# One layer of a hybrid attention block: the first two weight chunks laid out piece by piece, and the first input tile multiplied in two halves

## The chip, the cores and the metric

The kernel runs on one core of one Trainium2 chip. The metric is the device time of one execution in microseconds (us), the median over several runs; less is better. A profile of one execution shows what each engine did: PE is TensorE (PEld its weight loads), DVE VectorE, ACT ScalarE, POOL GpSimd, SP the engine that only issues transfers here. The engines run apart from each other and meet at semaphores; each takes its own instructions in a fixed order.

## What is computed

One layer for 512 frames of width 1024, in float32: a combined input projection, two kinds of attention, a gated mix, and a convolutional feed-forward part. The opening works on this piece of the reference:

```python
hn = rms_norm(x, norm1_g[l])
proj = hn @ w_in[l]
qa, ka, va = [proj[..., i * WIDTH_A:(i + 1) * WIDTH_A].reshape(b, s, N_HEADS_A, HEAD_DIM)
              for i in range(3)]
...
q = rms_norm(q, q_gain)
k = rms_norm(k, k_gain)
```

`w_in` has 1024 rows. A product over 1024 rows is summed over eight k tiles of 128 rows.

## The kernel before

**Precision.** Each float32 operand is split into a high part (rounded to the matmul's format) and a low part (the rest). A product takes three matmuls: high by high, high by low, low by high. For the input these parts are `hth` and `htl` (lines 385 and 386, ScalarE and VectorE, from `xs`), for weights `whi` and `wlo` (lines 278 to 281, from `raw`). In the trace `uA<-whi_uA,hth` is a matmul that adds to the bank uA with the weights' high part as moving data and the input's high part as stationary data.

**Chunks.** All weights are cut on the host into chunks of 128 x 2048 numbers (1 MB), in the order of their use (`_chunks`). The first two, `uA0` and `uA1`, hold the first four heads' columns of q and k: a chunk has four k tiles of 512 columns each, 256 of q and 256 of k. `uA0` has the k tiles 0 to 3, `uA1` 4 to 7. Then come `vA0`, `vA1` (the values), `qA1`, `kA1` and so on.

**Loading.** `load(i, parts)` issues a chunk's transfers on SP. In DRAM a chunk is `wts[i]`, 128 rows of 2048 numbers, 8 KB a row. A whole chunk goes as one transfer; the first two are loaded in four pieces of 512 columns (line 148), so that each partition takes 2 KB out of a row of 8 KB. The input is there transposed as `xt`, eight tiles of 128 x 512 (256 KB, contiguous). SP issues by turns one input tile (line 340) and one weight piece: xs 0, piece 0 of uA0, xs 1, piece 1, up to xs 7 and piece 3 of uA1. The rest of the parameters, the untransposed input `xtok` (2 MB, for the norms' factors) and the chunk `vA0` follow. A small load of the parameters that scale the input is issued on ScalarE's queue.

**Splitting.** `split_gen(i, pieces)` yields after each piece. The loop over k ahead of the first chunk takes one step of it for each input tile, so that the engines get, by turns, an input tile's parts and a weight piece's parts. The very first cast is VectorE's, all others are ScalarE's; all low parts are VectorE's. For later chunks `run_chunk` takes a step of the next chunk's split after each part of a chunk's matmuls. When a chunk is split, the load of the next but one is issued.

**Matmuls of the opening.** Nine warm-up matmuls on zeros (line 355) stand first on PE. Then `unit_groups` fills four banks of 128 frames x 512 columns (`pss[t]`, t = 0 to 3) from `uA0` and `uA1`. For `uA0` the k tile is the outer loop, then the three products, then the four banks: 12 matmuls of 512 columns for a k tile. For `uA1` the bank is the outer loop, and each bank is evacuated when it is full (`evac`: squares on ScalarE, a sum over 64 columns and factors on VectorE and GpSimd, then the normalized `n_uA`). `vA0` and `vA1` go the same way, through the same four banks; between their matmuls stand transposes of `n_uA` (line 574).

**Order.** The order of each engine's instructions is set when the program is built, by a scheduler with a model of time that takes ready work from several streams. A change of one instruction's size can so move others later on.

Of the kernel before, what the change touches and what calls it, by code (L numbers as in the profile page):

```python
# [8 lines left out]
F32 = mybir.dt.float32  # L9
F32R = mybir.dt.float32r  # L10
AF = mybir.ActivationFunctionType
ALU = mybir.AluOpType
# [3 lines left out]
P = 128  # L16
S = 512
D = 1024
NT = S // P
# [44 lines left out]

CHUNKS = _chunks()

SEVEN = (6, 7, 9, 10, 11, 12, 13, 15, 17)
LIVE = (17,)
EXTRA_AT = (7, 10, 12)
# [4 lines left out]
def block_kernel(ctx: ExitStack, tc: tile.TileContext, x, xt, params, g2, rbx, wts, wd0, wd1, out):  # L74
    nc = tc.nc
    V, A, G, PE, SP = nc.vector, nc.scalar, nc.gpsimd, nc.tensor, nc.sync
# [42 lines left out]
    FIRST_DN = order.index("dn0_0")  # L119
    keep = {}  # L120

    def load(i, parts=1):
        if i == FIRST_DN + 2:

            raw = late["hp"].tile([P, 2048], F32, tag="ax9", name="raw_dn0_2")
        else:
            raw = wp.tile([P, 2048], F32, tag="raw", name=f"raw_{order[i]}")
        raws[i] = raw
        if i >= FIRST_DN:
            n = i - FIRST_DN  # L130
            if n < NP:
                SP.dma_start(raw, wd0[n])
            else:
                late["load"] = (SP.dma_start(raw[:, 0:1024], wd1[n - NP]),)
            yield
            return

        if is_seven(i) and i - pos["up0"] not in LIVE:
            n = SEVEN.index(i - pos["up0"])
            SP.dma_start(raw[:, 0:512], wts[i, :, 0:512])  # L140
            SP.dma_start(raw[:, 512:1024], parked[n, :, 0:512])
            SP.dma_start(raw[:, 1024:2048], wts[i, :, 1024:2048])
            yield
            return
        cuts = [0, *parts, 8] if isinstance(parts, tuple) else [8 * j // parts for j in range(parts + 1)]
        for a, b in zip(cuts, cuts[1:]):
            sl = slice(256 * a, 256 * b)
            SP.dma_start(raw[:, sl], wts[i, :, sl])
            yield

    def chain(kind, ins):
# [34 lines left out]
    def is_seven(i):  # L186
        return i < len(order) and order[i] in [f"up{j}" for j in SEVEN]

    def park_gen():

        for j in SEVEN:
            if j in LIVE:
                continue
            n = SEVEN.index(j)
            i = pos[f"up{j}"]
# [17 lines left out]
    def block_sums(i):  # L213

        b = raws[i].rearrange("p (b c) -> p b c", c=512)
        sx = late["pool"].tile([P, 1536], F32, tag="sx", name=f"sx_{order[i]}")
        late["sx"] = sx
        s1, s2, s4 = (sx[:, 512 * j:512 * (j + 1)] for j in range(3))
        for o, x, y, op in ((s1, b[:, 1], b[:, 3], ALU.add), (s2, s1, b[:, 0], ALU.subtract),
                            (s4, b[:, 2], s2, ALU.subtract), (b[:, 1], b[:, 0], b[:, 1], ALU.subtract)):  # L220
            V.tensor_tensor(o, x, y, op=op)
            yield

    def fetch_extra(j):

        n = SEVEN.index(j)
        if j in EXTRA_AT:
            wh, wl = (t[:, 16:1552] for t in late["w2"])
        else:
            wh, wl = (late["pool"].tile([P, 1600], F32R, tag=tag, name=f"{tag}_up{j}")[:, 16:1552]  # L230
                      for tag in ("wxh", "wxl"))
        SP.dma_start(wh.bitcast(F32), parked[n, :, 512:2048])
        SP.dma_start(wl.bitcast(F32), parked[n, :, 2048:3584])
        extras[j] = wh, wl
# [21 lines left out]
    def split_gen(i, pieces):  # L256

        if i >= len(order):
            return
        key = order[i]  # L260
        kn = CHUNKS[i][1]
        raw = raws.pop(i)
        if i - pos["up0"] in LATE and i - pos["up0"] not in LIVE:
            fetch_extra(i - pos["up0"])
        sh = 48 if key[:2] in ("qA", "kA", "vB") else 16 if key in ("up0", "up1") or is_seven(i) else 0
        n = 512 * kn if i >= FIRST_DN else 2048
        hi = wp.tile([P, 2112], F32R, tag="whi", name=f"whi_{key}")[:, sh:sh + n]
        lo = wp.tile([P, 2112], F32R, tag="wlo", name=f"wlo_{key}")[:, sh:sh + n]
        splits[key] = (hi.rearrange("p (k c) -> p k c", k=kn), lo.rearrange("p (k c) -> p k c", k=kn))
        if i >= FIRST_DN:  # L270
            yield from split_down(i - FIRST_DN, raw, hi, lo)
        elif is_seven(i):
            yield from split_seven(i, raw, hi, lo)
        n = 2048 // pieces
        for j in range(pieces if i < FIRST_DN and not is_seven(i) else 0):
            sl = slice(n * j, n * (j + 1))
            if i == 0 and j == 0:
                V.tensor_copy(hi[:, sl], raw[:, sl])
            else:
                A.copy(hi[:, sl], raw[:, sl])  # L280
            V.tensor_tensor(lo[:, sl], raw[:, sl], hi[:, sl].bitcast(F32), op=ALU.subtract)  # L281
            if j < pieces - 1:
                yield


        nxt = {0: None, 1: i + 3, 2: None}.get(i - FIRST_DN, i + 2)
        if nxt is not None and nxt < len(order):
            next(load(nxt))
        j = i + 1 - pos["up0"]
        if j in SEVEN and j not in LATE:  # L290
            fetch_extra(j)
        yield
        if j in LIVE:
            yield from block_sums(i + 1)
# [17 lines left out]
    hth = hp.tile([P, NK, S], F32R, tag="hth", name="hth")  # L312
    htl = hp.tile([P, NK, S], F32R, tag="htl", name="htl")
# [21 lines left out]

    pieces = (p for i in range(2) for p in load(i, 4))
    for k in range(NK):
        SP.dma_start(xs[:, k, :], xt[k])  # L340
        next(pieces)
    for _ in pieces:
        pass
    SP.dma_start(par[:, 8:N_PAR], params[:, 8:N_PAR])
# [9 lines left out]
    for i in range(WARM):  # L354
        PE.matmul(pw.rearrange("p (a b) -> p a b", a=4), warm, warm.unsqueeze(1).to_broadcast([P, 4, P]),
                  start=True, stop=True)
# [70 lines left out]
    def unit_groups(hi, lo, key, evac):  # L427

        unit, half = key[:-1], int(key[-1])
        if half == 0:  # L430
            open_banks[unit] = [(MM if t else PV)(f"{unit}_{t}") for t in range(NT)]
        pss = open_banks[unit]

        def mm(t, k, j):
            st, mv = ((hth, hi), (hth, lo), (htl, hi))[j]
            PE.matmul(pss[t], st[:, 4 * half + k, t * P:(t + 1) * P], mv[:, k, :], start=half == 0 and k == 0 and j == 0,  # L436
                      stop=half == 1 and k == 3 and j == 2, skip_group_check=True)
        if key == "uA0":
            for k in range(4):
                for j in range(3):  # L440
                    for t in range(NT):
                        mm(t, k, j)
                yield
            return
        for t in range(NT):
            for k in range(4):
                for j in range(3):
                    mm(t, k, j)
            if half == 1:
                evac(t, pss[t])  # L450
            yield
# [387 lines left out]
    for s in range(len(steps)):  # L839
# [8 lines left out]
        br, h, t, e = pend.pop(0)  # L848
# [33 lines left out]
    n = 0  # L882
# [67 lines left out]
    hi, lo = splits.pop("wo3")  # L950
# [401 lines left out]
def _layout(inputs):  # L1352
    import numpy as np
    f = {k: np.asarray(v) for k, v in inputs.items()}
    x = f["x"]
    g = f["q_norm_g"][0]
    k = f["k_norm_g"][0]
    params = np.concatenate([
        f["norm1_g"].reshape(NK, P), np.concatenate([g, g])[None], np.concatenate([k, k])[None],
        f["ffn_conv_w"].reshape(3 * 2 * NF, P), f["ffn_conv_b"].reshape(2 * NF, P)], axis=0).T  # L1360

    idx = np.clip(np.arange(639) - 127, -128, 128) + 128
    rbx = f["rel_bias"][0][:, idx]
    wts = np.empty((len(CHUNKS) - 2 * NP, P, 2048), np.float32)
    for i, (key, kn, parts) in enumerate(CHUNKS[:-2 * NP]):
        views = [f[name][0][r0:r0 + kn * P, c0:c0 + n] for name, r0, c0, n in parts]
        w = views[0] if len(views) == 1 else np.concatenate(views, axis=1)
        if key in [f"up{j}" for j in SEVEN]:

            a = w.reshape(2, 4, P, 2, P).transpose(0, 3, 2, 1, 4)  # L1370
            wts[i] = np.concatenate([a[k, f].reshape(P, 512) for k in range(2) for f in range(2)], axis=1)
            continue
        wts[i] = w.reshape(kn, P, 2048 // kn).transpose(1, 0, 2).reshape(P, 2048)

    w = f["w_ffn_down"][0].reshape(NP, 2, P, 2, 512)
    wd0 = np.concatenate([w[:, 0, :, 0], w[:, 1, :, 0], w[:, 0, :, 1], w[:, 1, :, 1]], axis=2)
    wd1 = np.concatenate([w[:, 1, :, 1], w[:, 1, :, 0]], axis=2)
    arrays = {"x": x, "xt": x[0].T.reshape(NK, P, S),
              "params": params, "g2": f["norm2_g"], "rbx": rbx, "wts": wts, "wd0": wd0, "wd1": wd1}
    return {n: np.ascontiguousarray(a) for n, a in arrays.items()}  # L1380
# [15 lines left out]
```

## Time and profile before

| | us |
|---|---|
| median of 3 runs | 722.66 |
| the three runs | 721.46, 722.66, 722.86 |
| the profiled execution | 721.76 |
| its span, first to last instruction | 720.1 |
| PE busy | 712.3 |
| VectorE busy | 588.6 |
| ScalarE busy | 409.7 |

The span is 1.7 us shorter than the profiled execution's own time; that rest lies around the instructions. Busy time of PE is the sum of matmuls as recorded; matmuls overlap a little, so it is no measure of distance from the peak. In rows of a timeline the columns are: start, length, engine, line, operation, output and inputs, shape, count, and in brackets the engine's idle time ahead of it with what ended it. In rows of a window: the window, then busy time of PE, PEld, DVE, ACT and POOL (with counts), the granted clock of PE, the mean busy share of the DMA engines, and what they moved in GB/s, which is also KB per us. Rows of transfers give destination and source, the issuing queue, the count, the size of one, and the median us from issue to landing.

### The profile page before, as it was taken

How to read it: one execution, taken by the hardware profiler on the slowest of the kernel's cores; microseconds unless marked ns; L12 is line 12 of the kernel's file. 1: busy time of each engine (PE TensorE's matmuls, PEld its weight loads, DVE VectorE, ACT ScalarE, POOL GpSimd, SP SyncE). 2: the span in 40 equal slices, each digit the busy share in tenths (PEclk: the TensorE clock that was granted, in tenths of full speed). 3: DMA queues.
4: the chain of work that ended last, by engine and by line, in shares of the span. 5: the costliest groups of instructions: out<-in, count | busy, mean ns of one | idle time of the engine just before them, and what ended most of it. 6: DMA issues, size and time to landing. Idle time of an engine off the chain costs nothing.

```text
span 720.1 us, 10786 instructions
## 1 busy us (share of the span) xinstructions
PE 712.3 (99%) x3971; PEld 619.0 (86%) x3971; DVE 588.6 (82%) x1050; ACT 409.7 (57%) x755; POOL 54.9 (8%) x91
## 2 busy tenths in 40 slices
PE   8999999999999999999999999999999999999997
PEld 6889998888988888878889988999988988888885
DVE  6668878796998999869556698998999985998686
ACT  6666656667776677545335554666655543543531
POOL 2501200000110111100003000000000100000000
PEclk9999999999999999999999999999999999999999
DMA  9722235434434443554937837667765633564553
GB/s 303 269 106 88 76 129 187 179 133 180 157 148 160 176 162 147 192 190 172 335 124 287 264 117 257 247 230 289 250 248 204 227 130 115 185 244 167 181 214 117
DMA packets 38469, 136.59 MB, mean 190 GB/s; under 512 B 4112, under 2 KB 8592, under 8 KB 30864
## 3 DMA queue, kind: packets, MB, share of 16 engines
q1 hardware_dynamic: 35472, 122.66, 47.7%
q0 software_dynamic: 2656, 13.11, 4.9%
q8 instruction: 31, 0.51, 0.3%
q14 instruction: 22, 0.18, 0.1%
q10 hardware_dynamic: 288, 0.14, 0.1%
HBM read 109.41 MB, written 26.48 MB: 189 GB/s over the span
## 4 chain that ended last, share of the span: by engine, by line
PE 96%; DVE 2%; DMA 1%; ACT 0%; issue 0%; SPq 0%; DVEq 0%; ACTq 0%
PE P L1232 15%; PE p L1138 12%; PE pg L309 3%; PE pg L307 3%; PE pg L308 3%; PE pu L309 3%; PE pu L307 3%; PE pu L308 3%; PE uA L436 3%; PE vA L436 3%; PE qkB L309 2%; PE gB L307 2%; PE qkB L307 2%; PE qkB L308 2%; PE gB L308 2%; PE gB L309 2%
## 5 line engine op out<-in xcount | busy, mean ns | idle before, releaser
L1232 PE MATMUL P<-whi_dn,ax 128*128 128x512 f32 x176 | 54.4, 389 | 0.0
L165 ACT CAST whi_dn<-raw_dn 128x1024 fp32r<-128x1024 f32 x33 | 34.4, 1052 | 25.4 <-PE P L1232 11.1
L161 DVE TENSOR_TENSOR wlo_dn<-raw_dn,whi_dn 128x1024 fp32r<-128x1024 f32 x33 | 40.0, 1223 | 7.7 <-ACT whi_dn L165 7.7
L309 PE MATMUL pg<-hth,wlo_up 128*128 128x512 f32 (+1 forms) x120 | 43.3, 361 | 0.0
L307 PE MATMUL pg<-hth,whi_up 128*128 128x512 f32 (+1 forms) x120 | 43.2, 361 | 0.0
L308 PE MATMUL pg<-htl,whi_up 128*128 128x512 f32 (+1 forms) x120 | 43.2, 360 | 0.0
L308 PE MATMUL pu<-htl,whi_up 128*128 128x512 f32 (+1 forms) x116 | 41.6, 359 | 0.0
L307 PE MATMUL pu<-hth,whi_up 128*128 128x512 f32 (+1 forms) x116 | 41.6, 359 | 0.0
L309 PE MATMUL pu<-hth,wlo_up 128*128 128x512 f32 (+1 forms) x116 | 41.6, 358 | 0.0
L1232 PE MATMUL P<-whi_dn,ay 128*128 128x512 f32 x132 | 40.8, 389 | 0.0
L1232 PEld LDWEIGHTS P<-whi_dn,ax 128*128 128x128 f32 x176 | 33.0, 188 | 6.8
L207 ACT CAST pkh<-pkr 128x512 fp32r<-128x512 f32 x24 | 14.9, 621 | 38.5 <-DMA parked<-pkh 16.5
L281 DVE TENSOR_TENSOR wlo_up<-raw_up,whi_up 128x1024 fp32r<-128x1024 f32 (+1 forms) x32 | 31.3, 1022 | 4.7 <-ACT whi_up L280 4.7
L1232 PE MATMUL P<-wlo_dn,ax 128*128 128x512 f32 x88 | 34.2, 389 | 0.0
L280 ACT CAST whi_up<-raw_up 128x1024 fp32r<-128x1024 f32 (+1 forms) x32 | 26.5, 886 | 10.6 <-PE pu L308 5.8
L741 POOL TENSOR_SCALAR_AFFINE_SELECT bB<-bB 128x128 f32<-128x128 f32 x32 | 18.7, 592 | 151.6 <-DVE bB L740 132.3
L1232 PEld LDWEIGHTS P<-whi_dn,ay 128*128 128x128 f32 x132 | 24.8, 188 | 5.1
L739 DVE TENSOR_TENSOR_SCAN aB<-aB,reset 128x127 f32<-128x127 f32 (+3 forms) x32 | 25.7, 815 | 4.1 <-ACT aB L734 4.1
L208 DVE TENSOR_TENSOR pkr<-pkr,pkh 128x512 fp32r<-128x512 f32 x24 | 16.5, 687 | 12.3 <-ACT pkh L207 12.3
L307 PE MATMUL gA<-hth,whi_gA 128*128 128x512 f32 x64 | 25.5, 399 | 0.3 <-DVE mixA L619 0.3
L1232 PE MATMUL P<-wlo_dn,ay 128*128 128x512 f32 x66 | 25.8, 391 | 0.0
L1138 PE MATMUL p<-ts,whi_up 128*128 128x256 f32 x144 | 25.5, 277 | 0.0
(317 smaller groups left out, 2395.3 us busy)
## 6 DMA issues: line engine op xcount, KB each, us to landing
raw_up<-in_wts SPq DMA_DIRECT2D x14, 1024.0 KB, 5.2
raw_dn<-in_wd SPq DMA_DIRECT2D x11, 1024.0 KB, 4.8
pkr<-in_wts SPq DMA_DIRECT2D x8, 1024.0 KB, 6.7
parked<-pkr SPq DMA_DIRECT2D x32, 256.0 KB, 2.9
parked<-pkh SPq DMA_DIRECT2D x24, 256.0 KB, 2.0
raw_dn<-in_wd SPq DMA_DIRECT2D x11, 512.0 KB, 3.3
ayd<-ay POOLq DMA_DIRECT2D x7, 768.0 KB, 6.2
ay<-ayd POOLq DMA_DIRECT2D x7, 768.0 KB, 6.0
```

The lines of the kernel that those rows point to most:

```text
L161: chain("halves", V.tensor_tensor(o, x, y, op=op))
L165: chain("casts", A.copy(hi[:, sl], src))
L280: A.copy(hi[:, sl], raw[:, sl])
L281: V.tensor_tensor(lo[:, sl], raw[:, sl], hi[:, sl].bitcast(F32), op=ALU.subtract)
L307: PE.matmul(ps, sh, mh, start=first, stop=False)
L308: PE.matmul(ps, sh, ml, start=False, stop=False)
L309: PE.matmul(ps, sl, mh, start=False, stop=last)
L436: PE.matmul(pss[t], st[:, 4 * half + k, t * P:(t + 1) * P], mv[:, k, :], start=half == 0 and k == 0 and j == 0, stop=half == 1 and k == 3 ...
L739: V.tensor_tensor_scan(ar, ar, reset[:, S - n:S - 1][:, ::-1], 1.0, op0=ALU.mult, op1=ALU.max)
L741: G.affine_select(b[:, n - P:n], b[:, n - P:n], pattern=[[-1, P]], compare_op=ALU.is_gt, fill=0.0, base=0, channel_multiplier=1)
L1138: PE.matmul(ps, st, mv[:, k, :], start=first and k == 0 and n == 0, stop=last and k == 3 and n == 2, skip_group_check=True)
L1232: chain("products", PE.matmul(dst, st, mv, start=first and n == 0, stop=last and n == 2, skip_group_check=True))
```

## The change

Three things are changed. On the host, the numbers of chunks 0 and 1 are laid out in DRAM piece by piece, each piece contiguous (`CUTS` has the cuts). `load` reads each piece as one contiguous region; the row that a partition takes has 2 KB as before. The first piece of chunk 0 is cut in two, the 256 columns of q and the 256 columns of k of k tile 0, each a transfer of its own (128 KB, 1 KB for a partition); SP issues both behind the first input tile. Split and matmuls follow: VectorE casts the q half, ScalarE the k half, VectorE makes two low parts; and the matmuls of k tile 0 have 256 columns, 24 in place of 12, in the order high q, high k, low q, input's low part with q, with k, low k. All other chunks are loaded and split as before.

```diff
+CUTS = ((0, 256, 512, 1024, 1536, 2048), (0, 512, 1024, 1536, 2048))
...
-    def load(i, parts=1):
+    def load(i):
...
-        cuts = [0, *parts, 8] if isinstance(parts, tuple) else [8 * j // parts for j in range(parts + 1)]
-        for a, b in zip(cuts, cuts[1:]):
-            sl = slice(256 * a, 256 * b)
-            SP.dma_start(raw[:, sl], wts[i, :, sl])
+        for c0, c1 in zip(CUTS[i], CUTS[i][1:]) if i < 2 else ((0, 2048),):
+            src = bass.AP(wts.tensor, (2048 * i + c0) * P, [[c1 - c0, P], [1, c1 - c0]])
+            SP.dma_start(raw[:, c0:c1], src)
             yield
...
-        for j in range(pieces if i < FIRST_DN and not is_seven(i) else 0):
-            sl = slice(n * j, n * (j + 1))
+        cuts = CUTS[0] if i == 0 else [n * j for j in range(pieces + 1)] if i < FIRST_DN and not is_seven(i) else ()
+        for j, sl in enumerate(map(slice, cuts, cuts[1:])):
             if i == 0 and j == 0:
                 V.tensor_copy(hi[:, sl], raw[:, sl])
             else:
                 A.copy(hi[:, sl], raw[:, sl])
-            V.tensor_tensor(lo[:, sl], raw[:, sl], hi[:, sl].bitcast(F32), op=ALU.subtract)
-            if j < pieces - 1:
-                yield
+                if i == 0 and j == 1:
+                    yield
+                    V.tensor_tensor(lo[:, 0:256], raw[:, 0:256], hi[:, 0:256].bitcast(F32), op=ALU.subtract)
+            if (i, j) != (0, 0):
+                V.tensor_tensor(lo[:, sl], raw[:, sl], hi[:, sl].bitcast(F32), op=ALU.subtract)
+                if j < len(cuts) - 2:
+                    yield
...
-    pieces = (p for i in range(2) for p in load(i, 4))
+    pieces = (p for i in range(2) for p in load(i))
     for k in range(NK):
         SP.dma_start(xs[:, k, :], xt[k])
         next(pieces)
+        if k == 0:
+            next(pieces)
...
         if key == "uA0":
-            for k in range(4):
+            for j, c in ((0, 0), (0, 256), (1, 0), (2, 0), (2, 256), (1, 256)):
+                for t in range(NT):
+                    st, mv = ((hth, hi), (hth, lo), (htl, hi))[j]
+                    PE.matmul(pss[t][:, c:c + 256], st[:, 0, t * P:(t + 1) * P], mv[:, 0, c:c + 256],
+                              start=(j, c) == (0, 0), stop=False, skip_group_check=True)
+            yield
+            for k in range(1, 4):
...
+        if i < 2:
+
+            wts[i] = np.concatenate([wts[i][:, a:b].ravel() for a, b in zip(CUTS[i], CUTS[i][1:])]).reshape(P, 2048)
```

Where the instructions now stand, at three places. In the rows below, L is a line of the kernel that the rows belong to, the name ahead of the arrow is written and those behind it are read; the number at a name's end tells buffers apart.

VectorE in the opening, before: the cast of the first weight piece, the first input tile's low part, that piece's low part, and the next two.

```order
L278 CAST whi_uA_159<-raw_uA_119 128x512
L386 SCALAR_TENSOR_TENSOR htl<-xs,par,hth 128x512
L281 TENSOR_TENSOR wlo_uA_160<-raw_uA_119,whi_uA_159 128x512
L386 SCALAR_TENSOR_TENSOR htl<-xs,par,hth 128x512
L281 TENSOR_TENSOR wlo_uA_160<-raw_uA_119,whi_uA_159 128x512
```

And in the changed kernel:

```order
L279 CAST whi_uA_160<-raw_uA_119 128x256
L284 TENSOR_TENSOR wlo_uA_161<-raw_uA_119,whi_uA_160 128x256
L393 SCALAR_TENSOR_TENSOR htl<-xs,par,hth 128x512
L286 TENSOR_TENSOR wlo_uA_161<-raw_uA_119,whi_uA_160 128x256
L393 SCALAR_TENSOR_TENSOR htl<-xs,par,hth 128x512
L286 TENSOR_TENSOR wlo_uA_161<-raw_uA_119,whi_uA_160 128x512
```

Cast and low part of the first piece are halved; the q half's low part stands ahead of the input's low part, the k half's behind it.

ScalarE in the opening, before: two input tiles, then the second weight piece's cast.

```order
L95 DMA par<-in_params 128x8
L96 ACT_TABLE_LOAD
L385 ACTIVATE hth<-xs,par 128x512 x2
L280 CAST whi_uA_159<-raw_uA_119 128x512
L385 ACTIVATE hth<-xs,par 128x512
```

In the changed kernel the k half's cast stands between the first two input tiles:

```order
L97 DMA par<-in_params 128x8
L98 ACT_TABLE_LOAD
L392 ACTIVATE hth<-xs,par 128x512
L281 CAST whi_uA_160<-raw_uA_119 128x256
L392 ACTIVATE hth<-xs,par 128x512
L281 CAST whi_uA_160<-raw_uA_119 128x512
```

So the second input tile's part (and with it everything behind it on ScalarE) now waits for the k half too.

VectorE where uA's banks are evacuated and vA0 is split, before: `n_uA` is a bank's normalized q and k, `wlo_vA_306` the low parts of vA0 in four pieces, `ss_uA` a sum of squares.

```order
L466 TENSOR_TENSOR n_uA<-uA_221,rs_uA_301 128x2x256
L281 TENSOR_TENSOR wlo_vA_306<-raw_vA_175,whi_vA_305 128x512
L403 TENSOR_SCALAR cols<-cols 128x1
L281 TENSOR_TENSOR wlo_vA_306<-raw_vA_175,whi_vA_305 128x512 x3
L466 TENSOR_TENSOR n_uA<-uA_222,rs_uA_325 128x2x256
```

And in the changed kernel, where the pieces are `wlo_vA_321`:

```order
L479 TENSOR_TENSOR n_uA<-uA_224,rs_uA_316 128x2x256
L286 TENSOR_TENSOR wlo_vA_321<-raw_vA_180,whi_vA_320 128x512
L410 TENSOR_SCALAR cols<-cols 128x1
L286 TENSOR_TENSOR wlo_vA_321<-raw_vA_180,whi_vA_320 128x512
L475 TENSOR_REDUCE ss_uA_360<-sq_uA_358 128x8
L286 TENSOR_TENSOR wlo_vA_321<-raw_vA_180,whi_vA_320 128x512
L479 TENSOR_TENSOR n_uA<-uA_225,rs_uA_340 128x2x256
L286 TENSOR_TENSOR wlo_vA_321<-raw_vA_180,whi_vA_320 128x512
```

A sum of squares and the second bank's normalization moved ahead of the last pieces. Shifts of this kind, with the same instructions in another order, go on for PE, VectorE and ScalarE through the first attention heads, and end at the first matmuls of the chunk `kA1`; from there on the orders agree to the end. GpSimd's order is the same, and SP's has the one more transfer.

## The prediction

> **What bounds the kernel now.** I read the page's table of busy time first, then its chain that ended last, then the waits of the matmul engine over the whole span. They say that TensorE is the bound nearly everywhere, and that the opening is the one place where it stands still for long.
>
> ```profile
> PE 712.3 (99%) x3971; PEld 619.0 (86%) x3971; DVE 588.6 (82%) x1050; ACT 409.7 (57%) x755; POOL 54.9 (8%) x91
> ...
> PE 96%; DVE 2%; DMA 1%; ACT 0%; issue 0%; SPq 0%; DVEq 0%; ACTq 0%
> ...
> PE uA L436 <- DVE whi_uA L278: 1.3, 1, 1.3
> PE warm L355 <- DVE warm L352: 1.1, 1, 1.1
> PE yB L308 <- DVE ol_B L793: 0.4, 1, 0.4
> ```
>
> The reader is to see that after the opening no single wait of PE is longer than 0.4 us. So what the opening gains or loses is handed on to the end almost whole: every later engine and load follows PE, and PE has no slack of its own. Next comes the chain in order of time, in its first pieces.
>
> ```profile
> 0.80 0.39 SPq L340
> ...
> 1.25 4.82 DMA raw_uA<-in_wts
> 6.08 0.44 DVE whi_uA L278
> 6.52 0.14 issue
> 6.66 22.30 PE uA L436 x96
> ```
>
> The first 256 KB of weights are issued at 1.25 and land at 6.07; a VectorE copy of 0.44 and 0.14 of hand-over follow, and PE starts its first useful matmul at 6.66. From there its 96 matmuls of uA run through. The timeline of PE shows what lies ahead of that start and how the first k tile goes:
>
> ```profile
> 1.11 4.21 PE L355 MATMUL warm<-warm 128*128 128x512 f32 x9 [1.11 <-DVE warm L352]
> ...
> 4.69 0.63 PE L355 MATMUL warm<-warm 128*128 128x512 f32 x1
> ...
> 6.66 1.18 PE L436 MATMUL uA<-whi_uA,hth 128*128 128x512 f32 x4 [1.33 <-DVE whi_uA L278]
> 7.83 1.19 PE L436 MATMUL uA<-wlo_uA,hth 128*128 128x512 f32 x4
> 8.85 1.07 PE L436 MATMUL uA<-whi_uA,htl 128*128 128x512 f32 x4
> 9.76 1.07 PE L436 MATMUL uA<-whi_uA,hth 128*128 128x512 f32 x4
> ```
>
> Nine warm-up matmuls start from 1.11 to 4.69, (4.69 - 1.11)/8 = 0.45 us apart; those of uA start (9.76 - 8.85)/4 = 0.227 us apart. So PE runs at half pace at first and is at full pace later, whatever the page's row of granted clock (9 in every slice) says. The first k tile takes 9.76 - 6.66 = 3.10 instead of 12 x 0.227 = 2.72, since its second group waits for VectorE. The second k tile starts at 9.76: this is the mark by which I measure.
>
> The timelines of ScalarE and VectorE give what the first k tiles wait for.
>
> ```profile
> 3.69 0.72 ACT L385 ACTIVATE hth<-xs,par 128x512 fp32r<-128x512 f32 x1 [1.17 <-DMA par<-in_params]
> 6.79 0.73 ACT L385 ACTIVATE hth<-xs,par 128x512 fp32r<-128x512 f32 x1 [2.38 <-DMA xs<-in_xt]
> 8.29 0.62 ACT L280 CAST whi_uA<-raw_uA 128x512 fp32r<-128x512 f32 x1 [0.77 <-DMA raw_uA<-in_wts]
> ...
> 6.08 0.43 DVE L278 CAST whi_uA<-raw_uA 128x512 fp32r<-128x512 f32 x1 [5.02 <-DMA raw_uA<-in_wts]
> 6.43 0.75 DVE L386 SCALAR_TENSOR_TENSOR htl<-xs,par,hth 128x512 fp32r<-128x512 f32 x1
> 7.09 0.69 DVE L281 TENSOR_TENSOR wlo_uA<-raw_uA,whi_uA 128x512 fp32r<-128x512 f32 x1
> ```
>
> The first input tile is ready at 3.69 + 0.72 = 4.41, so only the weights are late. The next input tile lands at 6.79 and the next weight piece at 8.28.
>
> **The change part by part.** *When the weights land.* Three views bear on it: landing times of the first transfers, the same of line 140 (later in the kernel, 256 KB cut as 2 KB out of rows of 8 KB like today's pieces, ahead of its group), and the bytes moved in each microsecond.
>
> ```profile
> xs<-in_xt SPq DMA_DIRECT2D x1, 256.0 KB, 2.7
> raw_uA<-in_wts SPq DMA_DIRECT2D x1, 256.0 KB, 4.8
> ...
> L140 SPq DMA_DIRECT2D raw_up<-in_wts x8: 328/332/333, 424.1 to 510.9; - x8
> ...
> DMA to landing us min/median/max: 3.4/4.0/6.4
> ...
> 2.00:3.00 1.00, 1.00 (x4) 0.71 (x4) 0.00 (x0) 0.52 (x1) 0.93 (x2) 1.00 0.76 235
> 3.00:4.00 1.00, 1.00 (x4) 0.81 (x3) 0.00 (x0) 0.32 (x1) 0.94 (x2) 1.00 1.31 222
> 4.00:5.00 1.00, 1.00 (x4) 0.50 (x2) 0.00 (x0) 0.41 (x1) 0.67 (x2) 1.00 0.69 113
> 5.00:6.00 1.00, 0.32 (x1) 0.00 (x0) 0.00 (x0) 0.00 (x0) 0.00 (x0) 1.00 1.01 213
> 6.00:7.00 1.00, 0.34 (x2) 0.32 (x3) 0.92 (x2) 0.21 (x1) 0.00 (x0) 1.00 0.99 324
> ```
>
> The input tile, contiguous in DRAM, lands 2.7 after its issue, at 3.50. Cut pieces of the same size need 3.4 at best, 4.0 in the middle and 6.4 at worst. And while the first cut piece is under way the DMA engines are busy (0.69 to 1.31) but move 113 to 222 KB per us, against 324 later: they wait inside packets. I take it that the cut layout costs this. Contiguous, 128 KB behind the input tile's 256 KB at 222 KB per us land at 3.50 + 0.6 = 4.1; the bounds are 3.9 (at 324) and 6.07 (nothing gained). The second half follows by 4.7. The next input tile and weight piece bring the sum to 1049 KB; today 1107 KB have moved between 2.00 and 7.00, so these land by about 7.2, if no DMA engine lags, against 8.28.
>
> Of the Trainium skill a rule speaks against this: Perfetto Trace Analysis, Contiguity and DMAs, holds that contiguity counts only within one SBUF partition's line, and that is 2 KB before and after for all pieces but the halved one. By that rule the landing stays as it is, which is the first rival below; the rows of line 140 against the input tile's speak against the rule, without settling it, since other transfers stand around them.
>
> *When PE starts.* With a landing at 4.1, the cast of half the columns costs between 0.43/2 and 0.43, and the hand-over 0.14: ready by 4.7 at the latest. But the ninth warm-up starts at 4.69, and PE takes its work in order: the first useful matmul starts at 4.69 + 0.45 = **5.14**. The warm-up is what is late next; the landing has some 0.4 us of slack behind it.
>
> *The first k tile.* 24 matmuls of 256 columns take the place of 12 of 512. Their pace comes from qA, the same operands at 256 columns: 13 matmuls in the chain, of which the first and last are
>
> ```profile
> 54.85 0.12 PE qA L307
> ...
> 56.27 0.12 PE qA L307
> ```
>
> 1.42/12 = 0.118 each, so 24 x 0.118 = 2.83, 0.11 more than 2.72. VectorE now makes low part, input's low part, low part; the low part of the first half is ready some 0.4 after its cast, and PE asks for it 8 matmuls after its start, so the wait inside the tile goes. PE is at half pace at 4.69 and at full pace by 8.85, and at which moment it changes no row shows. With the change at 5.14 nothing is lost, with the change at 6.66 (6.66 - 5.14)/2 = 0.76; I take the middle, 0.38. The tile ends at 5.14 + 2.83 + 0.38 = **8.35**. Bounds: 7.97 and 8.73. The second k tile needs its cast by then: a landing at 7.2, 0.62 and 0.14 give 7.96. That fits.
>
> A sentence of the Trainium skill, TensorE: Matmul & The Clock Gate, Part 1, puts the change of pace after a free-running window of about 3.4 us of activity, so from 1.11 on between 4.5 and 7.9: an estimate by that page loses up to (7.9 - 5.14)/2 = 1.4 instead of 0.76.
>
> *Costed at nothing.* One more issue on SP moves every later one back by 1.72 - 1.25 = 0.47:
>
> ```profile
> 1.25 0.42 SPq L148 DMA_DIRECT2D raw_uA<-in_wts  x1
> 1.72 0.42 SPq L340 DMA_DIRECT2D xs<-in_xt  x1
> ```
>
> These transfers wait behind others for longer than that; were they not to, the second input tile would land 0.47 later than worked out, and its slack (PE needs it at 8.35) covers it. ScalarE's one more cast and VectorE's one more subtraction stand in a stage where each needs about 1.4 us for a k tile and PE 2.72. The order of PE, VectorE and ScalarE also differs up to kA's first matmuls, a tenth of the span from its start; there PE waits for nothing now, so reordering can gain nothing there, and it may cost.
>
> **The sum.** 9.76 - 8.35 = **1.41** us (bounds 9.76 - 8.73 = 1.03 and 9.76 - 7.97 = 1.79). Against the profiled execution, 721.76: 720.35. That execution lies 0.90 under the median of 722.66, and the three runs spread over 1.4 us. If that spread comes from this same landing (line 140's spreads from 3.4 to 6.4), the change takes it away too and the time stays at 720.35; if not, it is 722.66 - 1.41 = 721.25. I take the middle: **720.8**.
>
> **The rivals.** *The layout gives nothing (0.23).* The cut rows are not what stalls the DMA engines; the second half lands at 6.07, the next piece at 8.28. PE has the q half early, but its matmuls of the k half stand second in its queue. Second half: 6.07 + ScalarE's cast of 0.4 + 0.14 = 6.61; 20 matmuls x 0.118 end at 8.97; the second k tile needs 8.28 + 0.62 + 0.14 = 9.04. Gain 9.76 - 9.04 = 0.72, time 722.66 - 0.72 = 721.94. For it: in 4 to 6 us contiguous input tiles are in the queue too, and the slow stretch holds them as well.
>
> *The gain is given back at vA (0.08).* In VectorE's new order a reduction and a normalization stand ahead of the last low part of vA0.
>
> ```profile
> 27.50 1.89 DVE L281 TENSOR_TENSOR wlo_vA<-raw_vA,whi_vA 128x512 fp32r<-128x512 f32 x3
> 29.30 0.68 DVE L466 TENSOR_TENSOR n_uA<-uA,rs_uA 128x512 f32<-128x512 f32 x1
> 29.90 1.27 DVE L462 TENSOR_REDUCE ss_uA<-sq_uA 128x8 f32<-128x512 f32 x2
> ...
> 31.33 0.39 PE L436 MATMUL vA<-wlo_vA,hth 128*128 128x512 f32 x1
> ```
>
> Today it is done at 29.39 and wanted at 31.33. Behind 0.68 + 0.64 it is done at 30.71. If PE comes 1.41 earlier and VectorE not, PE waits 30.71 - 29.92 = 0.79, and 0.62 of the gain is left: 722.04. Against it: VectorE's work there hangs on PE's uA banks and moves along.
>
> *The second half late: slower (0.04).* The matmuls of the k columns stand ahead of all others in the queue, so PE ends the first k tile no sooner than the second half's landing + 0.54 + 20 x 0.118 = landing + 2.90. It is slower than today from a landing at 6.86. With the longest landing among the weight pieces of the opening, 6.9 after issue,
>
> ```profile
> DMA to landing us min/median/max: 4.8/5.8/6.9
> ```
>
> it would land at 1.72 + 6.9 = 8.62, the tile end at 11.52, 1.76 later than now: 724.4.
>
> **How the numbers follow.** My forecast has 0.65, with a range of its own from 719.9 (full pace at once, spread gone: 721.76 - 1.79 = 719.97) to 721.6 (722.66 - 1.03). The layout rival reaches up to 721.94, the vA rival to 722.04; the range is 719.9 to 722.2. A measurement of this kernel can tell about 0.2%, 1.44 us, from no change: faster means under 721.22. Of my forecast some 0.50 lies under it, of the layout rival 0.03 (where the spread goes); slower is the last rival. So 0.53 faster, 0.43 the same, 0.04 slower.
>
> **What would show it.** In the new profile the first 256-column matmul should start at about 5.1 with no wait behind the warm-ups, the first weight piece land by 4.6, the second k tile start near 8.35, and the stretch from 3 to 6 us move over 250 KB per us. If the first landing is still near 6, the layout was not the cause. If the second k tile starts early but uA's last matmul does not end some 1.4 us before 28.96, the gain is lost between; if it does and the whole is not shorter, in the reordered stretch up to kA. I am wrong if the DMA engines still stall, or if PE stays at half pace past 6.7 us.

## The result, and the profile after

| | before | after |
|---|---|---|
| median of the runs | 722.66 (7 runs, 721.46 to 723.23) | 720.05 (7 runs, 719.62 to 721.15) |
| ratio, 95% interval | | 0.9971 [0.9961, 0.9982] |
| the profiled execution | 721.76 | 719.62 |
| its span | 720.1 | 717.9 |

The kernel is faster by 2.61 us at the median and by 2.14 us between the two profiled executions. The ratio, which is not the quotient of these two medians (0.9964), gives 2.1 us, with an interval from 1.3 to 2.8. Forecast were 720.8, a range of 719.9 to 722.2, and a gain of 1.41. The sign holds and the time lies in the range, near its low end.

The page of the profile after: the row of busy times, and the chain's shares by engine.

```profile
PE 711.6 (99%) x3983; PEld 619.6 (86%) x3983; DVE 588.6 (82%) x1051; ACT 410.0 (57%) x756; POOL 55.2 (8%) x91
...
PE 97%; DVE 2%; ACT 0%; issue 0%; DVEq 0%; ACTq 0%
```

DMA has left the chain; PE's busy time is much as it was. What went is a wait. The matmul engine's waits after:

```profile
PE warm L362 <- DVE warm L359: 1.1, 1, 1.1
PE yB L313 <- DVE ol_B L806: 0.4, 1, 0.4
```

The 1.3 us of uA on the first cast are gone, and no new wait is in its place. PE's timeline of the opening after:

```profile
1.12 4.21 PE L362 MATMUL warm<-warm 128*128 128x512 f32 x9 [1.12 <-DVE warm L359]
5.13 1.23 PE L449 MATMUL uA<-whi_uA,hth 128*128 128x256 f32 x8
6.19 0.64 PE L449 MATMUL uA<-wlo_uA,hth 128*128 128x256 f32 x4
6.67 1.12 PE L449 MATMUL uA<-whi_uA,htl 128*128 128x256 f32 x8
7.63 0.64 PE L449 MATMUL uA<-wlo_uA,hth 128*128 128x256 f32 x4
8.11 1.09 PE L443 MATMUL uA<-whi_uA,hth 128*128 128x512 f32 x4
```

The first useful matmul follows the warm-ups at 5.13, and the second k tile starts at 8.11, not 9.76. What the weights do is read from the casts that take them, on VectorE and on ScalarE:

```profile
4.17 0.65 DVE L279 CAST whi_uA<-raw_uA 128x256 fp32r<-128x256 f32 x1 [3.11 <-DMA raw_uA<-in_wts]
```

```profile
5.08 0.41 ACT L281 CAST whi_uA<-raw_uA 128x256 fp32r<-128x256 f32 x1 [0.40 <-DMA raw_uA<-in_wts]
6.52 0.72 ACT L392 ACTIVATE hth<-xs,par 128x512 fp32r<-128x512 f32 x1 [1.03 <-DMA xs<-in_xt]
7.32 0.62 ACT L281 CAST whi_uA<-raw_uA 128x512 fp32r<-128x512 f32 x1
```

The q half is there at 4.17 and the k half at 5.08. The next piece waits for nothing but ScalarE, so it had landed by 7.32. In the windows of the same stretch,

```profile
4.00:5.00 1.00, 1.00 (x4) 0.57 (x3) 0.80 (x2) 0.68 (x1) 0.67 (x2) 1.00 0.81 223
5.00:6.00 1.00, 1.00 (x8) 1.00 (x8) 1.00 (x3) 0.41 (x1) 0.00 (x0) 1.00 1.02 346
```

the DMA engines move 223 and 346 GB/s where they moved 113 and 213. In second profiles of the two kernels, used further down, it is 174 and 326 against 109 and 260.

Where the 2.14 us come from shows in the chain in order of time. Two pieces of it after: vA's first matmul, and the first long run of p, a 256-column product of the feed-forward part.

```profile
27.34 0.23 PE vA L443
...
446.62 14.63 PE p L1151 x129
```

And of before:

```profile
28.96 0.24 PE vA L436
...
448.32 14.86 PE p L1138 x129
```

At vA the gain is 28.96 - 27.34 = 1.62; from there to p both take the same, 419.28 and 419.36. Then the same 129 matmuls take 0.23 less. So the opening's gain travels 419 us almost unchanged, and some 0.4 us more come up behind 446 us, in matmuls that the change doesn't touch.

### The profile page after: what moved, and what is told of

It is laid out like the page before. It is cut to its first block, busy times and chain, and to the rows that moved or that the text cites. A ratio compares the mean times of both kernels' runs of the same rounds, so it can differ in the third digit from the quotient of the medians.

```text
span 717.9 us, 10814 instructions
## 1 busy us (share of the span) xinstructions
PE 711.6 (99%) x3983; PEld 619.6 (86%) x3983; DVE 588.6 (82%) x1051; ACT 410.0 (57%) x756; POOL 55.2 (8%) x91
## 4 chain that ended last, share of the span: by engine, by line
PE 97%; DVE 2%; ACT 0%; issue 0%; DVEq 0%; ACTq 0%
PE P L1245 15%; PE p L1151 12%; PE pg L313 3%; PE pg L312 3%; PE pg L314 3%; PE pu L313 3%; PE pu L314 3%; PE pu L312 3%; PE vA L443 3%; PE uA L443 3%; PE qkB L314 2%; PE gB L312 2%; PE qkB L312 2%; PE qkB L313 2%; PE gB L313 2%; PE gB L314 2%
```

## The experiments

Runs of each kernel were taken by turns with runs of the kernel before on the same chip. The first four (`layout_only`, `split_only`, `pitch`, `warm13`) were compared together, then three more (`pitch_8448`, `pitch_32k`, `early`), then `pitch_8192`, each comparison on another chip. The ratio alone is not enough here: the runs of the kernel before fall mostly into two groups, 720.7 to 721.8 and 722.0 to 723.9. In the upper one were 16 of 26 runs in the first comparison, 12 of 28 in the second and 4 of 13 in the third, so its median was 722.62, 721.47 and 721.36, and ratios of different comparisons can't be set side by side. So each kernel is also read by marks in its profile: the cast of the next weight piece on ScalarE, the start of the second k tile on PE, and the first vA matmul.

| kernel | rows of chunks 0, 1 | next piece | 2nd k tile | vA | profiled | median | ratio |
|---|---|---|---|---|---|---|---|
| before | 8 KB | 8.29 | 9.76 | 28.96 | 721.76 | 722.66 | |
| before_again | 8 KB | 7.83 | 9.50 | 28.70 | 721.06 | | |
| before_third | 8 KB | 8.04 | 9.31 | 28.51 | 720.90 | | |
| split_only | 8 KB | 8.73 | 9.40 | 28.75 | 721.42 | 721.05 | 0.9981 [0.9972, 0.9990] |
| split_again | 8 KB | 7.63 | 8.45 | 27.68 | 719.98 | | |
| pitch_8192 | 8 KB, apart | 8.28 | 8.96 | 28.30 | 722.08 | 720.66 | 0.9982 [0.9971, 0.9992] |
| pitch_8448 | 8.25 KB, apart | 7.02 | 8.86 | 28.12 | 721.01 | 720.38 | 0.9976 [0.9965, 0.9986] |
| pitch | 9.25 KB, apart | 7.01 | 8.32 | 27.55 | 719.72 | 720.08 | 0.9969 [0.9956, 0.9982] |
| pitch_32k | 32 KB, apart | 7.52 | 8.59 | 27.82 | 720.12 | 720.16 | 0.9979 [0.9970, 0.9989] |
| layout_only | contiguous pieces | 6.91 | 8.37 | 27.57 | 719.97 | 720.17 | 0.9971 [0.9961, 0.9982] |
| after | contiguous pieces | 7.32 | 8.11 | 27.34 | 719.62 | 720.05 | 0.9971 [0.9961, 0.9982] |
| after_again | contiguous pieces | 7.07 | 8.14 | 27.37 | 719.71 | | |
| early | contiguous pieces | 7.02 | 7.84 | 27.07 | 719.30 | 720.23 | 0.9978 [0.9969, 0.9987] |
| warm13 | contiguous pieces | 6.54 | 8.62 | 27.85 | 721.84 | 722.80 | 1.0008 [0.9997, 1.0019] |

Times are us; "apart" is a DRAM tensor of its own that holds only chunks 0 and 1.

**The layout alone.** The kernel before, with its four pieces and its matmuls, but the pieces of chunks 0 and 1 contiguous.

```diff
             sl = slice(256 * a, 256 * b)
-            SP.dma_start(raw[:, sl], wts[i, :, sl])
+            if i < 2:
+                n = 256 * (b - a)
+                src = bass.AP(wts.tensor, (2048 * i + 256 * a) * P, [[n, P], [1, n]])
+            else:
+                src = wts[i, :, sl]
+            SP.dma_start(raw[:, sl], src)
```

> The kernel before with chunks 0 and 1 contiguous by piece in DRAM and nothing else: four pieces of 512 columns, 12 matmuls of 512 columns for the first k tile, the order of every engine as before. If the cut rows stalled the DMA engines (layout theory): the first piece (256 KB, behind 256 KB of input) lands at 4.6 to 4.9 instead of 6.07, PE starts at 5.2 to 5.5, the second k tile at 8.3 to 8.6 instead of 9.76, the time falls by 1.1 to 1.4 us. If the split did it (rival): the piece lands near 6, the second k tile starts at 9.4 to 9.8, the time falls by 0 to 0.3 us.

VectorE's first cast and PE's first and second k tile:

```profile
4.32 0.62 DVE L283 CAST whi_uA<-raw_uA 128x512 fp32r<-128x512 f32 x1 [3.26 <-DMA raw_uA<-in_wts]
```

```profile
5.12 1.57 PE L441 MATMUL uA<-whi_uA,hth 128*128 128x512 f32 x4
6.53 1.09 PE L441 MATMUL uA<-wlo_uA,hth 128*128 128x512 f32 x4
...
8.37 1.07 PE L441 MATMUL uA<-whi_uA,hth 128*128 128x512 f32 x4
```

The whole first piece lands at 4.32, earlier than the 4.6 to 4.9 expected, and the warm-ups are what PE starts behind, as after the full change. PE waits for no weights up to the second k tile. Its first four matmuls take 6.53 - 5.12 = 1.41 where full pace gives 4 x 0.227 = 0.91: 0.50 goes to half pace. The ratio is that of the full change, with the same interval. The orders of the engines are those of before, so the reordering is worth nothing that shows.

**The halves alone.** The changed kernel's pieces, casts and orders, but read out of rows of 8 KB as before.

```diff
-            src = bass.AP(wts.tensor, (2048 * i + c0) * P, [[c1 - c0, P], [1, c1 - c0]])
-            SP.dma_start(raw[:, c0:c1], src)
+            SP.dma_start(raw[:, c0:c1], wts[i, :, c0:c1])
```

> The changed kernel with the old layout in DRAM: the halves of the first piece and all other pieces are cut out of rows of 8 KB; the order of every engine as in the changed kernel. Layout theory: the q half lands at 5.0 to 5.6 instead of 4.17, the k half near 6, the next weight piece near 8 instead of 7.31, and the second k tile starts at 8.8 to 9.1 instead of 8.11: the time lies 0.5 to 0.8 us under that of the kernel before. Split theory: landings as in the changed kernel within 0.3, second k tile at 8.1 to 8.4, time 1.5 to 2 us under before.

> split_only once more, for a second profile: if its late pieces belong to the layout and not to one execution, the k half lands later than 5.4, the next weight piece later than 8.0, and the second k tile starts at 8.9 to 9.7; if they were one execution's, as in the changed kernel, 8.1 to 8.4.

VectorE's first cast and PE's timeline in the first of the two profiles:

```profile
4.46 0.35 DVE L278 CAST whi_uA<-raw_uA 128x256 fp32r<-128x256 f32 x1 [3.40 <-DMA raw_uA<-in_wts]
```

```profile
4.96 0.72 PE L448 MATMUL uA<-whi_uA,hth 128*128 128x256 f32 x4
6.12 0.74 PE L448 MATMUL uA<-whi_uA,hth 128*128 128x256 f32 x4 [0.44 <-ACT whi_uA L280]
...
9.40 1.20 PE L442 MATMUL uA<-whi_uA,hth 128*128 128x512 f32 x4 [0.64 <-ACT whi_uA L280]
```

PE starts early on the q half, then stands 0.44 for the k half and 0.64 for the next piece. That is the course of the rival "the layout gives nothing". The q half was expected at 5.0 to 5.6 if the layout sets its landing; out of rows of 8 KB it lands at 4.46, at 4.22 in the second profile and at 3.99 in the kernel on rows of 8192 B below, against 3.94 to 4.17 contiguous. So it is early by being half a piece, and the layout adds at most some tenths there; what it moves is the k half and the next piece. The second profile has the first wait at 0.28 and the second not at all, so its expected 8.9 to 9.7 was missed (8.45): the lateness differs between executions. With the kernel on rows of 8192 B below, which differs only in where these rows lie, the second k tile starts at 9.40, 8.45 and 8.96, mean 8.94: the halves alone gain 0.58 on the mean of before, 9.52, and the whole change 1.40.

**Is it contiguity?** Pieces cut out of longer rows, with chunks 0 and 1 in a tensor of their own; all else as in the halves alone. The numbers of filling a row, PAD, are 320, 64, 6144 or none; none of the filling is read. (With 320 it is copied from the rows and not zeros.)

```diff
-            SP.dma_start(raw[:, c0:c1], wts[i, :, c0:c1])
+            SP.dma_start(raw[:, c0:c1], wpd[i, :, c0:c1] if i < 2 else wts[i, :, c0:c1])
...
+              "wpd": np.concatenate([wts[:2], np.zeros((2, P, PAD), np.float32)], axis=2)}
```

> As split_only, but chunks 0 and 1 lie in DRAM in rows of 9472 bytes instead of 8192, so that the pieces are still cut out of longer rows, at a pitch that is no power of two. If it is the 8 KB pitch that stalls (rows that fall on the same part of DRAM): landings and second k tile as in the changed kernel (4.2 to 4.6, and 8.1 to 8.4). If any cut piece stalls (more DRAM touched for the same bytes): as split_only, second k tile at 8.8 to 9.1.

> As split_only, with rows of 8448 bytes in DRAM (8192 and 256 more). If the stall comes from rows that fall on the same part of DRAM at a pitch of 8 KB, and 256 bytes are enough to spread them: landings as with rows of 9472 bytes (q half near 4.0, k half near 5.0, next weight piece near 7.0), second k tile at 8.1 to 8.4, time about 2.5 us under before. If 256 bytes are too few: as split_only, k half after 5.5, next weight piece after 8.3, second k tile at 8.8 to 9.4.

> As split_only, with rows of 32768 bytes in DRAM: the dose doubled twice. If a pitch of a power of two is what stalls: landings at least as late as in split_only (k half 5.7 or later, next weight piece 8.7 or later), second k tile at 9.4 or later, time 0 to 1.5 us under before, or over it. If the stall has to do with the bytes between the pieces' rows being part of one 1 MB block, or is chance: landings like those of the changed kernel, second k tile at 8.1 to 8.4.

> The control for the three kernels with other row pitches: chunks 0 and 1 in the same separate DRAM tensor, but with rows of exactly 8192 B, so that a piece is cut out of rows of 8 KB as in the kernel before; halves and orders as in split_only. If the row pitch of 8192 B is what makes the pieces late: as split_only, k half landed near 5.7, next weight piece near 8.7, second k tile at 9.2 to 9.6, ratio about 0.998. If the place in the large tensor is (which holds all the chunks, where the separate tensor holds two): as the other pitches, k half landed by 5.6, next weight piece by 7.5, second k tile at 8.3 to 8.9, ratio about 0.997 to 0.998.

ScalarE's cast of the next piece with rows of 9472 B:

```profile
7.01 0.62 ACT L281 CAST whi_uA<-raw_uA 128x512 fp32r<-128x512 f32 x1 [0.28 <-DMA raw_uA<-in_wpd]
```

And with rows of 8192 B in the same separate tensor:

```profile
8.28 0.62 ACT L281 CAST whi_uA<-raw_uA 128x512 fp32r<-128x512 f32 x1 [0.63 <-DMA raw_uA<-in_wpd]
```

Rows of 9472 B are cut as before, yet the marks and the median are nearly those of contiguous pieces. Rows of 32768 B, where I had expected worse, come out between. Moving rows of 8192 B into another tensor didn't help: next piece at 8.28, second k tile at 8.96, under the 9.2 to 9.6 expected.

Over all fourteen profiles the six with rows of 8 KB have the next piece at 7.63 to 8.73, each after a wait for its transfer. The eight others, cut or contiguous, have it at 6.54 to 7.52, and only rows of 9472 B show such a wait there. So at the next piece the late ones are those cut out of rows of 8 KB; neither that they are cut nor the tensor they lie in makes them late.

The k half doesn't bear out that this holds for 8192 B alone. With rows of 8448 B ScalarE casts the k half and the next piece so:

```profile
5.61 0.41 ACT L281 CAST whi_uA<-raw_uA 128x256 fp32r<-128x256 f32 x1 [1.18 <-DMA raw_uA<-in_wpd]
...
7.02 0.62 ACT L281 CAST whi_uA<-raw_uA 128x512 fp32r<-128x512 f32 x1
```

Their k half lands at 5.61 and that of rows of 32768 B at 5.64, as late as out of rows of 8 KB (5.49 to 5.88); contiguous it lands by 5.18 at the latest, and out of rows of 9472 B at 5.05. With rows of 32768 B PE waits 0.42 for it, as much as in the halves alone. So the expectation for 8448 B came out mixed: its k half as if 256 B more were too few, its next piece as if they were enough. The row pitch matters, but no single rule tried here covers both marks, and with one profile a pitch the pitches other than 8192 B can't be ranked. What makes the difference the runs don't tell. The second k tile is no help with 8448 B: its 8.86 comes for the most part from half pace.

The Trainium skill, Perfetto Trace Analysis, Contiguity and DMAs, holds that contiguity counts only within a partition's line. Taken as a statement on contiguity it agrees with the rows of 9472 B at both marks (5.05 and 7.01); taken as a forecast for the layout it doesn't, since with 2 KB lines on both sides the first piece lands at 4.32 in place of 5.61 to 6.08.

**Is the start handed on to the end?** Thirteen warm-ups in place of nine.

```diff
-    WARM = 9
+    WARM = 13
```

> The changed kernel with 13 warm-up matmuls instead of 9. If the warm-ups set the start and nothing later has slack (prediction): PE starts about 0.9 to 1.3 us later (four matmuls of 512 columns at 0.227 to 0.43 each), at 6.0 to 6.4, the second k tile 0.8 to 1.1 us later than 8.11, and the time is longer than the changed kernel's by the same 0.8 to 1.1. If the landings of the pieces behind the first set the pace (rival): start later, but second k tile within 0.3 of 8.11 and time the same.

The second k tile starts 0.51 later (8.62), less than the 0.8 to 1.1 expected: the four more ran mostly at full pace. (The scheduler also moves some instructions up to the first attention heads.) But the profiled time, the shortest of this kernel's ten, is 2.2 longer. The matmul engine's wait that is new, and the piece of the chain ahead of it:

```profile
PE s_B L715 <- ACT bB L750: 1.0, 1, 1.0
```

```profile
192.68 0.63 ACT pkh L208
...
193.32 5.44 DMA parked<-pkh
```

ScalarE's next cast `pkh` waits for a 256 KB write of 5.44 us, ScalarE comes late to `bB`, and PE stands. From vA to p's long run this execution takes 420.98. The one with rows of 8192 B, in the changed kernel's orders, has the same wait (0.6) and takes 420.43; all twelve others take 419.24 to 419.36. So over this stretch a shift is handed on one to one, except in the two executions in which this write is slow; there 1.1 to 1.7 us are added. What makes it slow is open. A later start alone doesn't: the halves alone, in the same orders as the kernel on rows of 8192 B, reach vA later (28.75 against 28.30) and don't have the wait. And that one profiled execution, 722.08, is the slowest of its kernel's ten (719.58 to 722.08), so the others may well be without it.

**An earlier start.** Eight warm-ups, and four clears on VectorE in place of GpSimd, so that GpSimd's mask (`reset`) is done early.

```diff
-    WARM = 9
+    WARM = 8
...
-        G.memset(kl[64:128, 0, :].bitcast(F32), 0.0)
-        G.memset(kl[0:64, 1, :].bitcast(F32), 0.0)
+        V.memset(kl[64:128, 0, :].bitcast(F32), 0.0)
+        V.memset(kl[0:64, 1, :].bitcast(F32), 0.0)
```

> The changed kernel with 8 warm-ups instead of 9, and with four clears of 64 x 512 made by VectorE, which is idle there, instead of GpSimd, so that GpSimd's select of 128 x 512 is done by about 2.5 us and not at work from 4.06 to 4.67. If that select is what makes VectorE's first cast of 256 columns take 0.65 us (512 columns took 0.43 in the kernel before): the cast takes 0.2 to 0.35, PE starts at 4.7 to 4.8 instead of 5.13, the second k tile at 7.7 to 8.0, and the time falls by 0.1 to 0.4 us more. If not: cast 0.6, PE at 5.0 or later, time as the changed kernel's. In both cases the order of later instructions differs and may shift the time by some tenths.

The first cast takes 0.29 in place of 0.65:

```profile
3.96 0.29 DVE L279 CAST whi_uA<-raw_uA 128x256 fp32r<-128x256 f32 x1 [0.36 <-DMA raw_uA<-in_wts]
```

PE starts at 4.70 and the second k tile at 7.84, and this profile is the shortest of all (719.30). The median, 720.23 (719.30 to 721.47), can't be told from that of the changed kernel.

**Second and third profiles.** The kernels before and after once more, unchanged.

> The kernel before, looked at once more, for the spread of its opening. If the first landing varies from run to run (as that of line 140's transfers does, 3.4 to 6.4 us): first piece at 5.3 to 7.5, second k tile between 9.0 and 11.0, and the time differs from the other profiled execution by about as much as the second k tile's start. If the opening is steady: second k tile within 0.2 of 9.76, and the spread of the runs (721.46 to 723.23) comes from elsewhere.

> The kernel before once more, for a third profile: its times fall into a lower group, 720.7 to 721.8, where both of its profiles so far lie, and an upper one, 722.0 to 723.9. Theory: the upper group are executions in which ScalarE's cast pkh is held up by the write of the buffer parked near 195 us, which in two of the other kernels cost 0.6 to 1.0 us of waiting at the matmuls s_B and some 1.1 to 1.6 us of time. If this execution takes over 722.0, that wait of s_B on bB must stand among the matmul engine's waits, and the stretch from vA's first matmul to p's long one must take over 420 us in place of 419.3; if it takes over 722.0 without them, the theory falls. If it takes under 721.9, the stretch takes 419.2 to 419.5 and the theory stays untested.

> The changed kernel once more, for a second profile: if its early pieces belong to the layout, the q half is landed by 4.2, the next weight piece by 7.5, and the second k tile starts at 8.0 to 8.9, the later end with PE at half pace up to 6.7; if they were one execution's, it starts after 9.0. The feed-forward's last part (P) should start at 608.5 to 609.5 if the 0.35 us gained there was its own, 609.0 or later if not.

The three starts of the second k tile before are 9.76, 9.50 and 9.31, the two after 8.11 and 8.14: mean 9.52 against 8.13, 1.40 apart. The mean profiled times are 721.24 and 719.67, 1.57 apart. Between the first two profiles before the start differs by 0.26 and the time by 0.70, so the expectation that time follows the start alone was missed. The third profile fell into the lower group of times, so the theory that the upper group is the colliding write was not put to the test.

## Why the prediction was right, step by step

- **The landing** was forecast at 4.1 and is 4.17 (3.94 to 4.32 over all kernels with contiguous pieces). Right in the number, in part by luck. The prediction put it down to the contiguous layout, with 6.07 if that gains nothing; yet out of rows of 8 KB the q half lands at 3.99 to 4.46. Half the bytes bring it there, and a first piece landed by 4.6, named as the sign of the layout, couldn't tell the two apart. The layout shows in the whole first piece (4.32 against 5.61 to 6.08), in the k half and in the next piece. That any cut stalls the DMA engines was too wide as well: cut out of rows of 9472 B the pieces aren't late.
- **PE's start** at 5.14, right behind the warm-ups: 5.13. Right. The cast was priced at 0.43 at most and took 0.65; the slack of 0.4 covered it.
- **The second half** was to follow by 4.7 and came at 5.08, too late by 0.4. PE didn't wait for it: its first eight matmuls stand in one row without idle time. In the second profile it comes at 5.18, and PE's weight loads wait 0.2 for it. In the halves alone the same step costs 0.28 to 0.44.
- **The next piece** by about 7.2: ready by 7.32, 7.07 in the second profile. Right.
- **The first k tile** was to end at 8.35, bounds 7.97 and 8.73: 8.11 and 8.14. The term too large is the half pace, taken at 0.38. The first eight matmuls take 6.19 - 5.13 = 1.06 in place of 8 x 0.118 = 0.94, so 0.12 was lost. In the execution with rows of 8448 B the same eight take 1.82, 0.88 lost, of which some 0.1 is a wait for the k half (the fifth starts 0.31 behind the fourth, the first four 0.21 apart). The rest is as much as the bound of 0.76.
- **The gain** at the mark, 1.41 forecast, is 1.65 between the two profiled executions (0.24 from the half pace) and 1.40 between the means.
- **Nothing lost up to the end.** Right: 419.3 from vA to p in both. The rival "given back at vA" fell, there being no wait there.
- **The mis-sized step is the last one of the sum**, from the profiled execution to the median. I took half of its 0.90 as lying in the landing, so 720.8. The measured median has come down by 2.61, 0.96 more than the mark explains; the interval of the ratio, 1.3 to 2.8, leaves open how much of this is real. The start did spread over the three profiles before, but by 0.45 (9.31 to 9.76), not by 1.4. The rest fits the upper group of the runs before, which held five of its seven here, from 722.56 to 723.23. Moved by the mark's 1.65 that group would lie from 720.91 to 721.58, and one of the seven runs after, 721.15, lies there. So the group all but went with the change, which is why the time is near the low end of the range, but nothing shows that it went by way of the landing. That the slow write near 193 us makes the upper group is plausible, since it was seen in two other kernels and its price has the size, but no profile of before shows it.
- **The profile's other 0.4 us** were not foreseen. p's first 129 matmuls take 14.63 in ten of the fourteen profiles, two of those of before among them, and 14.86 to 15.24 in before, split_only, pitch_8192 and pitch_8448. It comes and goes with executions; what makes it no run shows.

What each part is worth: the layout alone brings the whole ratio. The halves on top of it show 0.23 to 0.26 at the mark (8.37 to 8.14 and 8.11), but that is no gain of theirs that is shown: PE waits for no weights in the layout alone, and its execution lost 0.50 to half pace in the first four matmuls where the changed kernel's lost 0.12 in the same work. At equal pace 24 matmuls are 0.11 longer than 12. The medians (720.17 and 720.05) don't tell the two apart either.

## What to carry to other kernels

Where a kernel starts by waiting for its first weights, look at the bytes moved in that stretch: DMA engines that move a third of their later rate (here 113 of 324 GB/s) are a reason to try another layout of the source rows, and a contiguous first piece, or another row pitch, is a change in one transfer. One such window proves nothing: rows of 8448 B moved only 73 GB/s from 4 to 5 us and still had the next piece by 7.02. Change one thing at a time, too: here the layout alone did what layout and halves did together. Once the wait is gone, the next fixed thing sets the start (here the warm-ups), so price the gain up to that and no further. Take a second profile of the kernel before ahead of arguing from its run-to-run spread: here the landing spread by 0.45 us, the runs by about 1.8.

## What the runs showed of the hardware that was not expected

**A cast that waits without a wait.** The 256-column first cast begins at 3.94 to 4.46 and ends at 4.81 or 4.82 in all nine profiles where GpSimd's mask stands in its old place, taking 0.35 to 0.87. GpSimd's timeline in the changed kernel has

```profile
4.06 0.61 POOL L330 TENSOR_SCALAR_AFFINE_SELECT reset<-reset 128x512 f32<-128x512 f32 x1
```

which ends at 4.67. With the mask done at 2.40, the cast takes 0.29. The Trainium skill, SBUF — State Buffer, SBUF: two separate sides, says that VectorE, in some kinds of instruction, and GpSimd share a pair of ports that one instruction holds to its end. The trace agrees in that the cast, whenever it begins, ends some 0.15 behind the mask; it counts as busy while it stands. That it is the ports, no run shows.

**Pace of PE.** The profile's granted clock reads 1.00 from the first window on, yet PE starts at half pace, and the change to full pace moves between executions: 13 warm-ups take 4.80 in one and nine take 4.21 in another, and with rows of 8448 B half pace lasts until 6.9,

```profile
5.12 1.98 PE L449 MATMUL uA<-whi_uA,hth 128*128 128x256 f32 x8
6.94 0.65 PE L449 MATMUL uA<-wlo_uA,hth 128*128 128x256 f32 x4
```

eight matmuls in 6.94 - 5.12 = 1.82 us, 0.228 each in place of 0.118, the wait of some 0.1 for the k half included.
